# A hybrid retention and attention layer on one core: w_out's split pieces and the gate's vector-matrix product dealt out anew over the heads of the first sequence

## The chip, the core and the metric

One NeuronCore of a Trainium2 chip runs the whole program; the other cores are idle. The metric is the device time of one execution in microseconds (us), and the kernel before is given as the median of three runs. One further execution was profiled; all rows below are of that one. The engines are called as in the profile: PE is TensorE (matmuls; PEld is its weight load), DVE is VectorE, ACT is ScalarE, POOL is GpSimd, SP is SyncE, which here only issues transfers.

## What is computed

Two sequences, `x_prompt` (1024 tokens) and `x_sample` (512 tokens), pass through one layer with shared weights, in fp32. Cut to what matters here:

```python
mod = silu(c) @ w_ada + b_ada
shift, scale, gate = split(mod, 3)
h = rms_norm(x, norm_g) * (1 + scale) + shift
rq, rk, rv, rg, aq, ak, av, ag = split(h @ w_in)
ret_out = bidirectional_retention(rope(rq), rope(rk), rv, ...)
att_out = blocked_gqa(rope(norm(aq)), rope(norm(ak)), av)
mixed = concat([ret_out * silu(rg), att_out * silu(ag)]) @ w_out
y = x + gate * mixed
```

The two things that the change concerns are the last third of `mod`, the row `gate` (a vector of 1024 times a 1024 x 1024 part of `w_ada`, for both sequences at once), and the preparation of `w_out` (1024 x 1024).

## The kernel before

**Products in three parts.** A product in fp32 is made of three faster ones: each operand is split into a high part and a remainder (`hi`, `lo`), and `mm3` (lines 148 to 151) adds high x high, high x low and low x high in PSUM. A split of weights is a copy that rounds (line 139: ACT for `w_in`; line 143: POOL, through `pcopy`, for `w_out`) and a subtraction (line 140: POOL and DVE in turn for `w_in`, DVE for `w_out`).

**Order.** `sequence(1, 4, True)` runs the 512-token sequence first, then `sequence(0, 8, False)` the long one. In the first, the four retention heads 0 to 3 come one after another, and as a fifth turn (head 4) the key, value and first query projections of the attention. In turn `h` the projection of head `h` (`pqk`, `pvg`; 2 x 4 steps of 24 matmuls) is woven with the core of head `h - 1`, `ret_core`: state products `pst` from `vds`, transposes `pk` and `pq`, decayed queries `qd0s` and `qd1s` on DVE (line 716), scores `psc` and `sTs` (line 725), the output product `pos` (line 739), its norm (`sqs`, `sss`, then POOL's root `r_rets`, line 127), `mxs` (line 748) and the transposes of `mxs` (`pms`). Before a head's products can be used, its rotary products `rt1s` and `rt2s` on DVE are added by POOL (line 637).

**The gate's row.** `gate_mod` (lines 240 to 255) is a generator of 16 steps. Each loads a piece of `w_ada` of 256 KB, `gr`, through SP (line 247) into a ring of four raw buffers, and issues two matmuls (four as the profile counts them) into `pgm` (line 251). The weights of the next head, and of head 4, pass through the same ring. After eight steps half of the row is copied out by ACT (line 254). The table `GSTEPS` (line 314) says how many steps are taken in each turn; one extra step ends the generator. The row is first read by `load_gate`, at the end of head 4.

**w_out.** `split_wo` (lines 173 to 185) prepares one of eight pieces: SP loads 512 KB into `wor` (two buffers; line 178, or two halves by line 182), POOL copies it rounded into `woz` (line 143; two buffers `z`, WZ = 2), DVE subtracts (line 140), and POOL issues the write of 1 MB to `wod` in DRAM (line 185). The output stages read `wod` back much later. `WOH` (line 36) gives the number of pieces whose code stands at the end of each turn:

```python
    if first and h < RH:
        for j in range(sum(WOH[:h]), sum(WOH[: h + 1])):
            with tc.issue_after(acts["w"].ins):
                split_wo(wst, j)
```

**What sets the order.** The order in which instructions stand on an engine is settled when the program is built, by a scheduler that goes by its own estimate of when operands are ready; `issue_after` only keeps a piece's instructions behind the last weight load issued. So a piece written at the end of turn 0 or 1 can be placed anywhere after that load, among the instructions of the next turn. At run time each engine, and SP's queue of transfers, goes through its instructions strictly in that order.

Of the kernel before, what the change touches and what calls it, by code (L numbers as in the profile page):

```python
# [32 lines left out]
KO = 7  # L33
OUTLAG = 0
WZ = 2
WOH = (0,1,3,4)
LEAD = 5
PLEAD = 3
PTURN = -7
# [41 lines left out]
def hybrid_layer_kernel(ctx: ExitStack, tc: tile.TileContext, a: dict, y_prompt: bass.AP, y_sample: bass.AP):  # L81
# [175 lines left out]
    def merge(p, n, q, m):  # L257
        done = 0
        for i in range(n):
            if p is not None:  # L260
                next(p, None)
            while done * n < (i + 1) * m:
                next(q, None)
                done += 1
                yield
            yield
        for z in (p, q):
            if z is not None:
                yield from z
# [9 lines left out]
    def weave(units, n, steps, m, lead=0):  # L279
        done = 0  # L280
        for i, _ in enumerate(units):
            while steps is not None and done * (n - lead) < (i + 1 - lead) * m:
                if next(steps, steps) is steps:
                    steps = None
                done += 1
        if steps is not None:
            for _ in steps:
                pass
# [22 lines left out]
    def behind_ada():  # L311
        return tc.issue_after(adma[-1].ins)

    GSTEPS = {1: 7, 2: 7, 3: 3}

    def sequence(r, nt, first):
        tg = "ps"[r]
# [3 lines left out]
        with ExitStack() as sctx:  # L321
# [176 lines left out]
            with ExitStack() as rctx:  # L498
# [261 lines left out]
                def gates(pl, tag):  # L760
                    gs.extend(slot(f"g{tg}{i}") for i in range(2 * ng))
                    for jj in range(2):
                        segs = [(2816 + v * 256 + (2 * jj + i) * DH, DH) for i in range(2) for v in range(2)]
                        w = load_w(wring, f"wg{tg}{jj}", segs)
                        for g in range(ng):
                            for i in range(2):
                                pj = bank(f"pag{tg}{g}{jj}{i}")
                                wc = slice(i * P, (i + 1) * P)
                                c = slice(i * 512, (i + 1) * 512)
                                for k in range(KD):  # L770
                                    mm3(pj, w[:, k, 0, wc], w[:, k, 1, wc], hh[g][:, k, :], hl[g][:, k, :],
                                        k == 0, k == KD - 1)
                                    if k == 3:
                                        yield
                                silu_gate(pl, gs[g * 2 + jj][:, c], pj, [512], f"a{tg}{g}{jj}{i}", tag, 1)
                                yield
# [18 lines left out]
                for h in range(RH + 1):  # L795
# [3 lines left out]
                    else:  # L799
# [3 lines left out]
                        else:  # L803
                            units, n = gates(rp, "rt1"), 8 * ng
                    extra, m = itertools.islice(gsteps, GSTEPS.get(h, 0)) if first else iter(()), nsteps
                    if first:
                        m += GSTEPS.get(h, 0)
                    weave(units, n, merge(prev, nsteps, extra, m - nsteps), m + ((2, 3)[r] if h == RH else 0))
                    if h == 0:
                        decay_tables()  # L810
# [3 lines that stand above are left out]
# [320 lines left out]
```

## Time and profile before

| | |
|---|---|
| median of 3 runs | 959.81 us (958.32 to 961.81) |
| profiled execution, its own time | 958.77 us |
| its span, first to last instruction | 957.0 us |
| mean granted TensorE clock | 0.996 |
| busy: PE, DVE, POOL, ACT | 95%, 56%, 36%, 35% |

How to read it: busy time is a share of the whole span, while the stages differ. The cores of the first sequence's heads end with the `pms` rows at 97.64, 133.44 and 168.73 us (turns 1 to 3) and one more in turn 4; behind that lie the attention and output of the first sequence and the whole of the second. A row of the timeline shows start, duration, engine, line, operation, `out<-in`, the number of instructions merged, and in brackets the idle time of the engine just before, with what ended it. Matmul durations overlap one another, so stretches of PE are read from start to start.

### The profile page before, as it was taken

How to read it: one execution, taken by the hardware profiler on the slowest of the kernel's cores; microseconds unless marked ns; L12 is line 12 of the kernel's file. 1: busy time of each engine (PE TensorE's matmuls, PEld its weight loads, DVE VectorE, ACT ScalarE, POOL GpSimd, SP SyncE). 2: the span in 40 equal slices, each digit the busy share in tenths (PEclk: the TensorE clock that was granted, in tenths of full speed). 3: DMA queues.
4: the chain of work that ended last, by engine and by line, in shares of the span. 5: the costliest groups of instructions: out<-in, count | busy, mean ns of one | idle time of the engine just before them, and what ended most of it. 6: DMA issues, size and time to landing. Idle time of an engine off the chain costs nothing. (4 is left out here: it accounts for less than half of the span.)

```text
span 957.0 us, 15488 instructions
## 1 busy us (share of the span) xinstructions
PE 909.4 (95%) x6177; PEld 761.0 (80%) x6177; DVE 539.0 (56%) x1006; ACT 336.2 (35%) x582; POOL 344.7 (36%) x312
## 2 busy tenths in 40 slices
PE   4889998999999899999999999999998999999998
PEld 2778898997666799999999998899865666666666
DVE  2465555677764593543525344344997767666633
ACT  4353232343545452232122232232144433343331
POOL 4233454365326453232302211135563434242330
PEclk9999999999999999999999999999999999999999
DMA  9964778223732511111102111010027001101111
GB/s 272 278 184 144 253 212 295 77 46 133 308 153 89 185 47 45 46 46 45 29 17 46 45 45 44 26 51 7 12 80 293 24 22 44 45 23 45 45 45 44
DMA packets 95684, 92.99 MB, mean 97 GB/s; under 512 B 23502, under 2 KB 84858, under 8 KB 92540
## 3 DMA queue, kind: packets, MB, share of 16 engines
q1 hardware_dynamic: 92876, 77.85, 26.6%
q0 software_dynamic: 2736, 14.16, 3.7%
q8 instruction: 48, 0.79, 0.3%
q14 instruction: 24, 0.20, 0.1%
HBM read 77.30 MB, written 14.68 MB: 96 GB/s over the span
## 5 line engine op out<-in xcount | busy, mean ns | idle before, releaser
L925 ACT ACTIVATE pp<-pTp 128x1024 f32<-128x1024 f32 x64 | 65.6, 1026 | 122.8 <-PE pTp L922 113.6
L933 POOL TENSOR_TENSOR accp<-accp,pp 128x512 f32<-128x512 f32 x48 | 62.5, 1303 | 126.6 <-ACT pp L925 124.7
L870 DVE TENSOR_REDUCE nmhp<-pnp 128x2 f32<-128x1024 f32 x64 | 76.0, 1217 | 45.6 <-PE pnp L865 45.6
L149 PE MATMUL pvgp<-wvgp,hhp 128*128 128x256 f32 x224 | 65.0, 290 | 0.0
L149 PE MATMUL pqkp<-wqkp,hhp 128*128 128x256 f32 x224 | 64.6, 288 | 0.0
L150 PE MATMUL pvgp<-wvgp,hhp 128*128 128x256 f32 x224 | 64.3, 287 | 0.0
L151 PE MATMUL pvgp<-wvgp,hlp 128*128 128x256 f32 x224 | 63.9, 285 | 0.0
L151 PE MATMUL pqkp<-wqkp,hlp 128*128 128x256 f32 x224 | 63.7, 284 | 0.0
L150 PE MATMUL pqkp<-wqkp,hhp 128*128 128x256 f32 x224 | 63.4, 283 | 0.0
L149 PE MATMUL pyp<-wo,Mhp 128*128 128x512 f32 (+1 forms) x136 | 54.3, 399 | 7.6 <-DVE xrp L1019 7.6
L942 PE MATMUL pop<-pp,VVp 128*64 128x512 f32 x256 | 58.7, 599 | 0.0
L150 PE MATMUL pyp<-wo,Mhp 128*128 128x512 f32 (+1 forms) x136 | 51.6, 379 | 0.0
L151 PE MATMUL pyp<-wo,Mlp 128*128 128x512 f32 (+1 forms) x136 | 51.6, 379 | 0.0
L933 DVE TENSOR_TENSOR accp<-accp,pp 128x512 f32<-128x512 f32 x48 | 38.6, 804 | 15.8 <-ACT pp L925 15.1
L637 POOL TENSOR_TENSOR sp<-rt1p,rt2p 128x512 f32<-128x512 f32 x16 | 22.9, 1429 | 57.7 <-DVE rt2p L634 57.7
L149 PEld LDWEIGHTS pqkp<-wqkp,hhp 128*128 128x128 f32 x224 | 43.0, 192 | 0.0
L150 PEld LDWEIGHTS pqkp<-wqkp,hhp 128*128 128x128 f32 x224 | 42.9, 192 | 0.0
L151 PEld LDWEIGHTS pqkp<-wqkp,hlp 128*128 128x128 f32 x224 | 42.9, 191 | 0.0
L149 PEld LDWEIGHTS pvgp<-wvgp,hhp 128*128 128x128 f32 x224 | 42.8, 191 | 0.0
L150 PEld LDWEIGHTS pvgp<-wvgp,hhp 128*128 128x128 f32 x224 | 42.8, 191 | 0.0
L151 PEld LDWEIGHTS pvgp<-wvgp,hlp 128*128 128x128 f32 x224 | 42.8, 191 | 0.0
L942 PEld LDWEIGHTS pop<-pp,VVp 128*64 128x64 f32 x256 | 16.9, 136 | 32.4 <-issue 27.9
(458 smaller groups left out, 2799.3 us busy)
## 6 DMA issues: line engine op xcount, KB each, us to landing
wo<-wod SPq DMA_DIRECT2D x16, 1024.0 KB, 14.9
wa<-in_w_ada_dram SPq DMA_DIRECT2D x16, 512.0 KB, 5.9
wod<-woz POOLq DMA_DIRECT2D x8, 1024.0 KB, 6.6
gr<-in_w_ada_dram SPq DMA_DIRECT2D x16, 256.0 KB, 4.9
xn<-in_x_prompt_dram SPq DMA_DIRECT2D x8, 512.0 KB, 7.0
xrp<-in_x_prompt_dram SPq DMA_DIRECT2D x8, 512.0 KB, 3.6
out_dram<-xrp POOLq DMA_DIRECT2D x7, 512.0 KB, 2.9
xs<-in_x_sample_dram SPq DMA_DIRECT2D x4, 512.0 KB, 5.8
```

Source lines behind the costliest of these rows:

```text
L149: T.matmul(out, lh, rh, start=first, stop=False)
L150: T.matmul(out, lh, rl, start=False, stop=False)
L151: T.matmul(out, ll, rh, start=False, stop=last)
L637: G.tensor_tensor(qk, t1, t2, op=ALU.add)
L870: V.tensor_reduce(d["nmh"][:, n, 2 * pr : 2 * pr + 2], pn.rearrange("p (i k) -> p i k", i=2), AX.X, ALU.max, negate=True)
L925: d["exp", u] = S.activation(p, pT, AF.Exp)
L933: d["sum", v] = E.tensor_tensor(acc, acc, p[:, i * 512 : (i + 1) * 512], op=ALU.add)
L942: m = T.matmul(d["po"][v * DH : (v + 1) * DH, :], VV[:, 2 * kp + i, v, :], ps[v][:, i * 512 : (i + 1) * 512], start=(kp + i == 0), stop=(2 ...
```

## The change

Two tables get other numbers:

```diff
-WOH = (0,1,3,4)
+WOH = (2, 2, 2, 2)
...
-    GSTEPS = {1: 7, 2: 7, 3: 3}
+    GSTEPS = {1: 4, 2: 6, 3: 7}
```

No instruction is added or left out. The code of w_out's pieces stands two by two at the ends of turns 0 to 3, where it stood as none, one, three and four; the gate's sixteen products are done four, six and six in turns 1, 2 and 3, where it was seven, seven and two. What the scheduler makes of that is shown at three places.

POOL, from the end of turn 0 into turn 1. In the names, `ss0_1` is the rotated q and k of head 0, second pair of tiles, `woz2` and `wor2` are w_out's third piece, `wqks2r0` is the first raw piece of head 2's weights. Before:

```order
L637 TENSOR_TENSOR ss0_0_759<-rt1s0_0_761,rt2s0_0_762 128x512
L143 TENSOR_SCALAR woz0_1190<-wor0_1188 128x2x512
L637 TENSOR_TENSOR ss0_1_760<-rt1s0_1_770,rt2s0_1_771 128x512
L185 DMA wod0_60<-woz0_1190 128x2048
L637 TENSOR_TENSOR ss1_0_816<-rt1s1_0_919,rt2s1_0_920 128x512
L140 TENSOR_TENSOR wqks2_1196<-wqks2r0_1197,wqks2_1196 128x2x256
L637 TENSOR_TENSOR ss1_1_817<-rt1s1_1_1002,rt2s1_1_1003 128x512
L140 TENSOR_TENSOR wqks2_1196<-wqks2r2_1207,wqks2_1196 128x2x256
L125 TENSOR_SCALAR m_rets0_0_1112<-sss0_0_1110 128x4
L127 TENSOR_TENSOR r_rets0_0_1114<-m_rets0_0_1112,mhalf_71 128x4
```

Changed, from its third such row on:

```order
L143 TENSOR_SCALAR woz1_824<-wor1_822 128x2x512
L637 TENSOR_TENSOR ss0_1_760<-rt1s0_1_770,rt2s0_1_771 128x512
L185 DMA wod0_60<-woz0_818 128x2048
L185 DMA wod0_60<-woz1_824 128x2048
L637 TENSOR_TENSOR ss1_0_828<-rt1s1_0_931,rt2s1_0_932 128x512
L143 TENSOR_SCALAR woz2_1191<-wor2_1188 128x2x512
L140 TENSOR_TENSOR wqks2_1204<-wqks2r0_1205,wqks2_1204 128x2x256
L637 TENSOR_TENSOR ss1_1_829<-rt1s1_1_1010,rt2s1_1_1011 128x512
L140 TENSOR_TENSOR wqks2_1204<-wqks2r2_1215,wqks2_1204 128x2x256
L185 DMA wod0_60<-woz2_1191 128x2048
L143 TENSOR_SCALAR woz3_1198<-wor3_1195 128x2x512
L185 DMA wod0_60<-woz3_1198 128x2048
```

Where one piece stood between head 0's rotary sums, two stand now; the third and the fourth stand inside turn 1, the third ahead of head 1's second sum, and behind these rows the fifth comes ahead of the root `r_rets`.

DVE in turn 1, from head 1's second rotary product to the scores `sTs0_0` of head 0. Before:

```order
L634 TENSOR_TENSOR rt2s1_1_1003<-pqks1_1_942,rs_739 128x128 x4
L140 TENSOR_TENSOR wqks2_1196<-wqks2r1_1202,wqks2_1196 128x2x256
L716 TENSOR_TENSOR qd0s0_0_1025<-pqs0_0_1012,QD_752 128x512
L716 TENSOR_TENSOR qd1s0_0_1027<-pqs0_0_1012,QD_752 128x512
L140 TENSOR_TENSOR wqks2_1196<-wqks2r3_1212,wqks2_1196 128x2x256
L725 TENSOR_TENSOR sTs0_0_1063<-pscs0_0_1058,DT_751 128x512
```

Changed:

```order
L634 TENSOR_TENSOR rt2s1_1_1011<-pqks1_1_950,rs_739 128x128 x4
L140 TENSOR_TENSOR woz2_1191<-wor2_1188,woz2_1191 128x2x512
L140 TENSOR_TENSOR wqks2_1204<-wqks2r1_1210,wqks2_1204 128x2x256
L140 TENSOR_TENSOR wqks2_1204<-wqks2r3_1220,wqks2_1204 128x2x256
L716 TENSOR_TENSOR qd0s0_0_1033<-pqs0_0_1020,QD_752 128x512
L716 TENSOR_TENSOR qd1s0_0_1035<-pqs0_0_1020,QD_752 128x512
L725 TENSOR_TENSOR sTs0_0_1067<-pscs0_0_1062,DT_751 128x512
```

w_out's third piece and a second split of head 2's weights have moved ahead of `qd0s` and `qd1s`.

SP at the end of turn 2 and into turn 3; `wvgs3r3` is the last raw piece of head 3's weights, `gr1..` a piece of the gate's second half, `wkvs` the weights of head 4, and what a transfer waits for stands in brackets. Before:

```order
L164 DMA wvgs3r3_1627<-in_w_in_dram 128x2x128
L178 DMA wor4_1941<-in_w_out_dram 128x2x512 [waits DMAHW0_49]
L178 DMA wor5_1947<-in_w_out_dram 128x2x512 [waits DMAHW1_49]
L247 DMA gr112_1662<-in_w_ada_dram 128x2x256 [waits DMAHW3_49,DMAHW2_49,DVE_49]
L247 DMA gr113_1741<-in_w_ada_dram 128x2x256 [waits Pool_49]
L164 DMA wkvsr0_1974<-in_w_in_dram 128x2x256 [waits DMAHW5_49,DMAHW4_49,Pool_49]
```

Changed:

```order
L164 DMA wvgs3r3_1623<-in_w_in_dram 128x2x128 [waits PE_49]
L164 DMA wvgs3r3_1623<-in_w_in_dram 128x2x128
L182 DMA wor6_1953<-in_w_out_dram 64x2x512 [waits DMAHW6_49]
L182 DMA wor6_1953<-in_w_out_dram 64x2x512 [waits DMAHW7_49]
L182 DMA wor7_1960<-in_w_out_dram 64x2x512 [waits DMAHW0_49]
L182 DMA wor7_1960<-in_w_out_dram 64x2x512 [waits DMAHW1_49]
L247 DMA gr102_1658<-in_w_ada_dram 128x2x256 [waits DMAHW2_49,DVE_49]
L247 DMA gr103_1705<-in_w_ada_dram 128x2x256 [waits DMAHW3_49,Pool_49]
L247 DMA gr110_1741<-in_w_ada_dram 128x2x256 [waits DMAHW5_49,DMAHW4_49,DVE_49]
L247 DMA gr111_1796<-in_w_ada_dram 128x2x256 [waits Pool_49]
L247 DMA gr112_1832<-in_w_ada_dram 128x2x256 [waits DMAHW6_49,DMAHW2_49,PE_49]
L247 DMA gr113_1888<-in_w_ada_dram 128x2x256 [waits DMAHW7_49,DMAHW3_49,PE_49]
```

Six gate transfers, not two, now stand behind w_out's last two pieces (before, its fifth and sixth; the last two stood further on, among head 4's weights). On POOL the copy of `wor6` stands ahead of the split that frees the raw buffer of `gr103`.

## Rows read from the trace of the kernel before

**Rows 1.** The page, its span and its busiest engines.
```profile
span 957.0 us, 15488 instructions
PE 909.4 (95%) x6177; PEld 761.0 (80%) x6177; DVE 539.0 (56%) x1006; ACT 336.2 (35%) x582; POOL 344.7 (36%) x312
```

**Rows 2.** Waits of PE, 44 to 240 us: total, times, longest.
```profile
PE pgm L251 <- DMA gr<-in_w_ada_dram: 3.7, 4, 1.2
PE pos L739 <- DVE qd1s L716: 3.2, 1, 3.2
```

**Rows 3.** Timeline of PE, heads 1 to 3 (start, duration, what; idle before).
```profile
70.12 1.06 PE L251 MATMUL pgm<-gr,scT 128*32 128x256 f32 x12
72.08 0.63 PE L251 MATMUL pgm<-gr,scT 128*32 128x256 f32 x4 [0.90 <-DMA gr<-in_w_ada_dram]
73.64 0.63 PE L251 MATMUL pgm<-gr,scT 128*32 128x256 f32 x4 [0.94 <-DMA gr<-in_w_ada_dram]
74.20 0.71 PE L693 MATMUL psts<-vds,ss 128*128 128x128 f32 x4
...
88.91 0.38 PE L739 MATMUL pos<-R1s,qd1s 128*128 128x128 f32 x2
...
97.64 0.27 PE L501 MATMUL pms<-identr,mxs 128*128 128x128 f32 x1
...
133.44 0.27 PE L501 MATMUL pms<-identr,mxs 128*128 128x128 f32 x1
...
139.65 0.61 PE L693 MATMUL psts<-vds,ss 128*128 128x128 f32 x4
...
159.09 0.49 PE L739 MATMUL pos<-R1s,qd1s 128*128 128x128 f32 x2 [3.19 <-DVE qd1s L716]
...
168.73 0.27 PE L501 MATMUL pms<-identr,mxs 128*128 128x128 f32 x1
```

**Rows 4.** Busy time by stretch; PEclk is third from the right.
```profile
160.40:163.80 3.40, 3.40 (x19) 3.40 (x18) 1.30 (x2) 0.00 (x0) 0.59 (x1) 0.50 0.82 273
```

**Rows 5.** Timeline of POOL, heads 1 to 3.
```profile
71.53 1.05 POOL L143 TENSOR_SCALAR woz<-wor 128x1024 fp32r<-128x1024 f32 x1 [3.62 <-DMA wor<-in_w_out_dram]
72.54 1.26 POOL L637 TENSOR_TENSOR ss<-rt1s,rt2s 128x512 f32<-128x512 f32 x1
...
102.20 3.50 POOL L140 TENSOR_TENSOR wvgs<-wvgs2r,wvgs 128x512 fp32r<-128x512 f32 x2
...
149.44 1.05 POOL L143 TENSOR_SCALAR woz<-wor 128x1024 fp32r<-128x1024 f32 x1 [3.75 <-DMA wor<-in_w_out_dram]
```

**Rows 6.** Timeline of DVE, heads 1 to 3.
```profile
84.91 0.68 DVE L716 TENSOR_TENSOR qd1s<-pqs,QD 128x512 f32<-128x512 f32 x1
...
99.55 0.69 DVE L140 TENSOR_TENSOR wvgs<-wvgs2r,wvgs 128x512 fp32r<-128x512 f32 x1 [0.60 <-ACT wvgs L139]
...
102.27 2.30 DVE L140 TENSOR_TENSOR woz<-wor,woz 128x1024 fp32r<-128x1024 f32 x1 [2.03 <-POOL woz L143]
...
107.19 1.23 DVE L140 TENSOR_TENSOR woz<-wor,woz 128x1024 fp32r<-128x1024 f32 x1 [0.94 <-POOL woz L143]
...
154.23 3.61 DVE L140 TENSOR_TENSOR wkvs<-wkvsr,wkvs 128x512 fp32r<-128x512 f32 x1
```

**Rows 7.** Timeline of ACT, head 1.
```profile
71.53 0.51 ACT L677 ACTIVATE vds<-ss,kd 128x256 f32<-128x256 f32 x1
```

**Rows 8.** Line 182 (`wor`), loads of a piece's halves.
```profile
DMA to landing us min/median/max: 3.7/5.4/7.1
```

**Rows 9.** Line 185 (`wod<-woz`), writes of a piece of 1 MB.
```profile
DMA to landing us min/median/max: 4.5/6.6/9.2
```

**Rows 10.** Busy time by stretch, `pvgs` alone, head 3: PE, PEld, DVE, ACT, PEclk.
```profile
165.00:168.60 3.60, 3.60 (x31) 3.60 (x31) 0.00 (x0) 0.00 (x0) 1.00 0.30 109
```

**Rows 11.** Timeline of SP, weights of head 1.
```profile
54.30 5.72 SPq L164 DMA_DIRECT2D wvgs1r<-in_w_in_dram  x8
```

**Rows 12.** Line 247 (`gr`), loads of the gate's pieces.
```profile
DMA to landing us min/median/max: 2.7/4.9/6.7
```

## The prediction

> **What bounds it now.** The page first: TensorE (PE) is busy 95% of the span and no other engine above 56% [rows 1]. A PE that is nearly always busy runs through its instructions in their fixed order, so only what makes it wait, or slows it, can move the end. The view of who waited for whom, limited to PE and to 44 to 240 us, therefore comes second [rows 2]: two entries there concern the change, the gate's products (`pgm`) waiting for their transfers `gr`, 3.7 us in four waits, and one product of the retention core (`pos`) waiting 3.2 us for `qd1s` from VectorE (DVE). Third, PE's timeline shows where they stand [rows 3]: 0.90 and 0.94 in head 1, so the other two, 1.87, in head 2; and 3.19 at 159.09, in head 3. Fourth, the granted clock [rows 4]: for 3.40 us behind that last wait it is 0.50, the lower level (1.2 GHz of 2.4); half of 3.40 is 1.7 us lost. What the change can take away is thus 1.84 + 1.87 + 3.19 + 1.7 = **8.6 us**.
>
> The other engines matter through queues that are strictly in order. On GpSimd (POOL) a piece of w_out that has not landed holds up all behind it: idle 3.62 us before 71.53 and 3.75 before 149.44 [rows 5]. DVE's subtraction for a piece takes 1.23 us by itself and 2.30 beside a POOL instruction [rows 6].
>
> **The change, part by part.** No instruction is added or dropped; places change. Base: the profiled execution, 958.77 us (957.0 of span and 1.8 around it), 1.04 below the median 959.81.
>
> *Gate products.* Each is four matmuls, 0.56 us (73.64 to 74.20 [rows 3]). Head 1 does four instead of seven, head 2 six instead of seven, head 3 six instead of two: the sum stays. In head 1 the products that run behind one another are three: 70.12 + 1.06 [rows 3], so 71.2, where now it is 74.20. PE then wants `vds`, which ScalarE starts at 71.53 and has at 72.05 (0.51 [rows 7]): PE waits 0.9.
>
> *w_out in heads 0 and 1.* The order shows two pieces before the second half of head 0's rotary sum on POOL, three more inside head 1, the sixth as head 2 begins. The first lands as now (71.53); 1.05 each for two copies (L143 [rows 5]), some 0.4 for the second transfer, and 1.26 for the sum at 72.54 [rows 5] end at 75.3; PE wants it at 75.1. So 0.2 more, **1.1** in all (bounds 0 and 2.8: 1.7 more, if the second piece lands in 7.1 instead of the median 5.4 [rows 8]).
>
> Third piece: its buffer `z` (two exist) is free when the first has been written out: issued at 75.3, 6.6 to landing [rows 9], about 82.0. POOL copies it to 83.05 and goes on without a pause: a split, a sum, a split. DVE must take the piece, then two splits, then `qd0s` and `qd1s`. Two engines that both read SBUF alternate here, as at 102.20 (two POOL splits in 3.50) against 102.27 (2.30) [rows 5, 6]: 83.05 + 1.26 + 1.23 + 1.26 + 0.69 (the split at 99.55) + 1.26 + 0.69 + 2 x 0.68 (84.91) = 90.8, with 1.26 (72.54) for each of POOL's. PE is there at 88.91 - 2.15 + 0.2 = 87.0, since it left 72.05 instead of 74.20. Wait: **3.8**. From below: landing in 4.5 [rows 9], nothing alternating: 0. From above: landing in 9.2, 6.4. I take the median landing, as no row ties a quick or slow one to this place.
>
> The row gives 6.6 us for writing out a piece of 1 MB. The Trainium skill ("DMA: Bandwidth & Descriptors", Anatomy of one DMA) gives such a transfer of GpSimd's 2.0 us plus its bytes over 436 GB/s, an estimate of 4.4; by it this wait would be 1.6 and the sum -0.3. The trace's quickest, 4.5, is about that, its median is not, and the measured one stands in the sum.
>
> After it PE needs 97.64 - 88.91 - 0.56 = 8.2 to the transposes of `mxs` (one product less): 99.0. There the fifth piece stands before `r_rets` on POOL; its transfer is issued behind the next weights at about 91.2, lands 5.4 later, 1.05 and 1.3 for copy and root, then `mxs`: 99.4. If the clock falls behind the wait of 3.8, as it did behind that of 3.19, PE comes at 100.7 by itself. Between the two I take 100.0, against 97.64 now: **1.0** is added (bounds 0 and 1.7).
>
> *Head 2.* Its four gate transfers wait for splits that now come some 2 us later; the first lands about when wanted: **0.5** (0 to 1.9, as now). 133.44 - 97.64 = 35.80, less 1.87, less 0.56, plus 0.5: head 3's start falls at 133.9, now 133.44 [rows 3].
>
> *Head 3.* The piece in mid-head goes: the 3.19 and the 1.7 with it. But the gate's transfers stand on SP behind w_out's seventh and eighth piece, and the second waits for a raw buffer that POOL frees only after it has copied the seventh piece, which it waits for. The last weights are issued when head 2's sixth product is done, 24 matmuls (at 31 in 3.60 us [rows 10], 2.8) and a product before 133.9: 130.5. Two issues at 0.7 (eight in 5.72 [rows 11]), the piece's two halves at 0.6, landing 5.4 after the second is issued: 137.9. Copy 1.05, split 1.26, landing 4.9 [rows 12]: 145.2. PE wants it at 133.9 + 6.2 (133.44 to 139.65 [rows 3]), 0.6 for the state products there, 0.8 for seven matmuls and 0.56 for the product before: 142.1. Wait, with the smaller one of the product before it: **3.1** (quickest landings 3.7 and 2.7: 0; slowest 7.1 and 6.7: 6.6). Further on, scores (`sTs`) and squares (`sqs`) stand behind splits of `wkvs`, whose loads also moved: 0 to 3.2 (nearest row: 159.09), I take **1.0**, as those loads have two more projections as cover. Without the clock falling: 168.73 - 133.44 = 35.29, less 4.9, plus four products 2.2, plus 4.1: head 4's first transpose at 170.6, now 168.73.
>
> At nothing: the later end of the gate's row, covered by the k, v and q products that stand before its first use in load_gate; w_out's writes, read back in the output stage only. If those covers went, a product (0.56) or a landing (6.6) would show.
>
> **Sum:** -8.6 + 1.1 + 3.8 + 1.0 + 0.5 + 3.1 + 1.0 = **+1.9**. Own time 960.7; on the median's footing **961.7**.
>
> **Rivals.** *The transfers are quick.* With landings of 4.5 for writes, 3.7 and 2.7 for reads, the new waits shrink to 1.1, 1.7 (3.8 less 2.1), 0, 0.5, 0 and 0.5, together 3.8, and 8.6 - 3.8 = 4.8 come back: **955.0**. For it: no wait is then longer than the gate's 1.2 now, behind which no clock falls [rows 2], and the pieces are spread more evenly. Against: medians, not minima, fit the rows so far. By the rule on the Trainium skill's page "DMA: Bandwidth & Descriptors" named above, this rival would be the likelier one.
>
> *Slower: the gate's second transfer in head 3.* If the seventh piece lands in 7.1 and the gate's transfer in 6.7, the wait is 6.6 instead of 3.1 and the clock falls behind it (1.7 [rows 4]): +1.9 + 3.5 + 1.7 = +7.1, **966.9**. It decides where the two landings together pass 12 us, above their medians' 10.3. For it: POOL's own 3.75 of idle before 149.44. Against: no gate transfer waits that long now. The Trainium skill ("TensorE: Matmul & The Clock Gate", Part 1) says that idleness takes the clock to its lower level, by which a wait of this size costs its own length and that fall; the trace shows it once, at 160.40.
>
> *The waits only change places.* The new ones equal the old and the time stays within 1 us: **959.8**; the fixed order of PE favours it, nothing ties the sums together.
>
> **Numbers.** Forecast 0.5, quick 0.2, slower 0.2, same places 0.1. A change under 0.3% (2.9 us) can't be told from none. Quick gives faster, 0.20. The forecast's own range, 958.5 to 966, lies a little more below +2.9 than above: 0.28 of its 0.5 is same, 0.22 slower. Same 0.28 + 0.1 = 0.38; slower 0.22 + 0.2 = 0.42. The range 954.5 to 968 reaches just past the centres of both rivals, and so leaves out about half of each.
>
> **What would show it.** Right: no wait for `qd1s` in head 3 and none for `gr` in head 1; a wait of `pos` for `qd1s` of some 3 us near 87 to 91, POOL idle before the third and the fifth piece, a wait for `gr` near 142. Wrong: `qd1s` in head 1 in time, or gate transfers of head 3 landing before 142; then PE is ahead of its present place at 168.73. An end that moves with none of these waits would break the argument altogether.

## The result, and the profile after

The changed kernel takes 965.68 us (median of 8 runs, 962.1 to 969.5) against 960.28 for the kernel before (median of 8 runs, 958.32 to 961.81): a ratio of 1.0062, 95% interval 1.0037 to 1.0087. It is slower. The profiled execution took 965.12 us (before: 958.77). So 6.35 us have to be found between the two traces.

The page of the changed kernel shows the same work on every engine as [rows 1], in a longer span:

```profile
span 963.3 us, 15491 instructions
PE 914.3 (95%) x6177; PEld 763.4 (79%) x6177; DVE 539.1 (56%) x1006; ACT 335.8 (35%) x582; POOL 344.8 (36%) x312
```

Waits of PE from 44 to 240 us (total, times, longest), to be held against [rows 2]:

```profile
PE pms L501 <- DVE mxs L748: 6.1, 1, 6.1
PE pos L739 <- DVE qd1s L716: 3.2, 1, 3.2
PE p0s L149 <- ACT hhs L507: 2.0, 2, 1.4
PE psts L693 <- POOL woz L143: 1.0, 1, 1.0
```

No wait for `gr` is left, in any head. A wait for `mxs` of 6.1, which the kernel before does not have, is now the longest. PE's timeline, the rows that answer to [rows 3]:

```profile
69.88 1.06 PE L251 MATMUL pgm<-gr,scT 128*32 128x256 f32 x12
71.91 0.68 PE L693 MATMUL psts<-vds,ss 128*128 128x128 f32 x4 [0.97 <-POOL woz L143]
...
90.13 0.49 PE L739 MATMUL pos<-R1s,qd1s 128*128 128x128 f32 x2 [3.16 <-DVE qd1s L716]
...
104.47 0.47 PE L501 MATMUL pms<-identr,mxs 128*128 128x128 f32 x1 [6.10 <-DVE mxs L748]
...
140.45 0.38 PE L501 MATMUL pms<-identr,mxs 128*128 128x128 f32 x2
...
147.64 0.62 PE L251 MATMUL pgm<-gr,scT 128*32 128x256 f32 x4
148.99 0.62 PE L251 MATMUL pgm<-gr,scT 128*32 128x256 f32 x4
...
165.71 0.38 PE L739 MATMUL pos<-R1s,qd1s 128*128 128x128 f32 x2
...
174.78 0.27 PE L501 MATMUL pms<-identr,mxs 128*128 128x128 f32 x1
```

Against 97.64, 133.44 and 168.73 the first `pms` rows of the three cores stand 6.83, 7.01 and 6.05 later, and the span ends 6.3 later. Net, the whole loss stands at 104.47; behind it, heads 2 and 3 together win 0.8 back, though the clock costs some 2.2 there (below). What made `mxs` late is in POOL's timeline:

```profile
82.13 1.05 POOL L143 TENSOR_SCALAR woz<-wor 128x1024 fp32r<-128x1024 f32 x1 [2.94 <-DMA wod<-woz]
...
100.56 1.03 POOL L143 TENSOR_SCALAR woz<-wor 128x1024 fp32r<-128x1024 f32 x1 [7.89 <-DMA wor<-in_w_out_dram]
101.67 1.24 POOL L125 TENSOR_SCALAR m_rets<-sss 128x4 f32<-128x4 f32 x1
102.99 1.04 POOL L127 TENSOR_TENSOR r_rets<-m_rets,mhalf 128x4 f32<-128x4 f32 x1
```

and in DVE's:

```profile
95.44 0.69 DVE L743 TENSOR_REDUCE sss<-sqs 128x4 f32<-128x512 f32 x1 [3.31 <-ACT sqs L741]
101.62 1.22 DVE L140 TENSOR_TENSOR woz<-wor,woz 128x1024 fp32r<-128x1024 f32 x1 [5.49 <-POOL woz L143]
104.06 1.13 DVE L748 SCALAR_TENSOR_TENSOR mxs<-pos,r_rets,ss 128x128 f32<-128x128 f32 x4 [1.21 <-POOL r_rets L127]
```

The sum `sss` is there at 96.13. The root that needs it comes at 102.99, because POOL stands idle for 7.89 us before the fifth piece's copy, which is ahead of the root in its fixed order. PE could have gone on at 98.37 (104.47 - 6.10). The loads of the fifth and the sixth piece were issued by SP from 91.90 on, behind head 2's weights. The view of that line has one landing there, of the sixth piece, issued at 92.94 (microseconds to landing: least, median, most); the fifth's is not recorded, but POOL's copy of it starts 8.7 us after its issue at 91.90:

```profile
DMA to landing us min/median/max: 8.8/8.8/8.8
```

The view of the transfers from 88 to 101 us says what they shared the engines with, the writes of the third and fourth piece among it: 3.95 MB, where the kernel before moved 1.77 MB in the same 13 us. After and then before:

```profile
DMA packets 2462, 3.95 MB, mean 304 GB/s; under 512 B 159, under 2 KB 1695, under 8 KB 2204
```

```profile
DMA packets 2096, 1.77 MB, mean 136 GB/s; under 512 B 132, under 2 KB 1606, under 8 KB 2095
```

The clock falls within the wait and is at its lower level behind it (PEclk third from the right; [rows 4] are the same columns), some 2.2 us lost: half of 104.47 to 108, and 0.23 of the next two.

```profile
104.00:106.00 2.00, 1.53 (x7) 1.53 (x8) 1.94 (x6) 0.00 (x0) 1.97 (x4) 0.50 0.46 197
106.00:108.00 2.00, 2.00 (x12) 2.00 (x11) 2.00 (x1) 0.00 (x0) 2.00 (x2) 0.50 0.80 328
108.00:110.00 2.00, 2.00 (x15) 2.00 (x15) 2.00 (x3) 0.27 (x1) 0.15 (x1) 0.77 0.12 12
```

### The profile page after: what moved, and what is told of

The parts are those of the page before. It is cut to its first block, busy times and chain, and to the rows that moved or that the text cites. A ratio compares the mean times of both kernels' runs of the same rounds, so it can differ in the third digit from the quotient of the medians.

```text
span 963.3 us, 15491 instructions
## 1 busy us (share of the span) xinstructions
PE 914.3 (95%) x6177; PEld 763.4 (79%) x6177; DVE 539.1 (56%) x1006; ACT 335.8 (35%) x582; POOL 344.8 (36%) x312
```

## The experiments

**Theory A:** what costs the time is the place of pieces in the fixed orders of POOL and DVE, ahead of work that PE is about to need (head 0's root first of all). **Theory B:** it is the crowd of pieces and transfers in head 1, whatever the order. **Theory C:** it is the gate's products in head 3.

Single runs of one kernel lie up to 8 us from their median, so beside the time each trace gives a **stretch**: from the start of head 1's merged gate products (70.12 before) to head 4's first state product (172.05 before, row below). Before it is 101.93 us, in the changed kernel 178.10 - 69.88 = 108.22: 6.3 of the 6.35. The stretch is that of the profiled run. That run lies within 2 us of its kernel's median except in e2 (957.82, 3.1 below), e6 (961.07, 4.1 above and the slowest of its 12) and e10 (965.74, 3.2 below). The ratio is to the runs of the kernel before on the same chip.

```profile
172.05 0.61 PE L693 MATMUL psts<-vds,ss 128*128 128x128 f32 x4
```

| run | pieces, gate's steps | order of turn 2's pieces | stretch | us, median | ratio to before, 95% interval |
|---|---|---|---|---|---|
| before | 0,1,3,4; 7,7,3 | as scheduled | 101.93 | 959.8 to 961.2 | |
| change | 2,2,2,2; 4,6,7 | as scheduled | 108.22 | 965.68 | 1.0062 (1.0037 to 1.0087) |
| e1 | 2,2,2,2; 7,7,3 | as scheduled | 103.41 | 959.52 | 0.9988 (0.9962 to 1.0014) |
| e2 | 0,1,3,4; 4,6,7 | as scheduled | 102.31 | 960.95 | 1.0016 (0.9993 to 1.0038) |
| e3 | 2,2,2,2; 4,6,7 | behind the root | 105.75 | 963.13 | 1.0038 (1.0018 to 1.0059) |
| e4 | the same, three `z` | as scheduled | 105.53 | 964.53 | 1.0044 (1.0016 to 1.0072) |
| e5 | 2,2,2,2; 4,6,7 | behind root and splits | 102.75 | 958.37 | 0.9999 (0.9971 to 1.0026) |
| e6 | 0,1,3,4; 4,6,7 | behind the root | 103.09 | 956.97 | 0.9966 (0.9942 to 0.9991) |
| e7 | 0,1,3,4; 4,6,7 | behind root and splits | 97.50 | 955.29 | 0.9955 (0.9929 to 0.9982) |
| e8 | 2,2,2,2; 4,6,7, three `z` | behind root and splits | 96.97 | 955.10 | 0.9957 (0.9938 to 0.9976) |
| e9 | 0,1,3,4; 7,7,3 | behind root and splits | 101.37 | 960.06 | 0.9998 (0.9974 to 1.0022) |
| e10 | change, once more | as scheduled | 108.28 | 968.94 | 1.0081 (1.0056 to 1.0106) |

**e1, the pieces alone.** Of the change only the `WOH` line.

```diff
-WOH = (0,1,3,4)
+WOH = (2, 2, 2, 2)
```

> The pieces of w_out go two to each head as in the change, the gate keeps its seven, seven and two products of before in heads 1, 2 and 3. In this order head 0's root (r_rets) stands ahead of the fifth piece on POOL; in the changed kernel it stands behind it. Theory A (the loss is that place: the root waits for a piece that lands late, 6.1 us at 104.47, and the clock falls behind it for some 1.9): no wait of pms for mxs above 1.5, no fall of the clock at 100 to 110; the qd1s wait of head 1 shrinks from 3.2 to about 1.0, because the three products come back there (2.1 us); about 957 us, 8 below the change and 3 below before. Theory B (the crowd of pieces and transfers in head 1 costs the time in whatever order): the waits only move, 963 or more. Theory C (the gate's products in head 3 cost it): about 957 as well, but then the kernel with the gate's part alone is slower than before in head 3, not in head 1.

The time is that of before, neither A's 957 nor B's 963. In head 1 A's account of the root holds: no wait for `mxs`, no wait for `qd1s`, root at 96.46 and the fifth piece at 103.55, behind it. What A did not foresee stands in two places. Head 1 opens with a wait for `gr`, and the clock is at its lower level behind it (0.50 from 76 to 78 us), some 1.7 us lost:

```profile
73.58 0.63 PE L251 MATMUL pgm<-gr,scT 128*32 128x256 f32 x4 [1.71 <-DMA gr<-in_w_ada_dram]
```

And in head 3, with the piece in mid-head gone, but only two products there, PE waits 1.17 for `qd1s` and then

```profile
164.74 0.49 PE L739 MATMUL pos<-ss,sTs 128*128 128x128 f32 x2 [2.72 <-DVE sTs L725]
```

**e2, the gate's steps alone.** Of the change only the `GSTEPS` line.

```diff
-    GSTEPS = {1: 7, 2: 7, 3: 3}
+    GSTEPS = {1: 4, 2: 6, 3: 7}
```

> The pieces of w_out stay where they were before (none, one, three, four), only the gate's products move. In this order POOL has two pieces (the second and the third) ahead of head 0's root, which before stood ahead of both. Theory A: their loads are issued behind head 2's weights near 92 and land near 97 to 101, so the root comes near 101 to 103 and mxs near 104; PE wants it near 95 to 96, waits 6 us or more, and its clock falls: head 2 begins some 5 to 8 us later than before, end 963 to 968. Theory B (the crowd of pieces in head 1): only one piece is copied there before the root's place, so no such wait: 957 to 960. Theory C (the gate's products in head 3): head 1 gains up to 2, head 3 loses, its qd1s wait of 3.2 and a wait for gr: 960 to 964 with the loss behind 135 us.

POOL, the second and third piece ahead of the root:

```profile
92.39 1.04 POOL L143 TENSOR_SCALAR woz<-wor 128x1024 fp32r<-128x1024 f32 x1 [7.33 <-DMA wor<-in_w_out_dram]
93.69 1.90 POOL L143 TENSOR_SCALAR woz<-wor 128x1024 fp32r<-128x1024 f32 x1 [0.26 <-DMA wor<-in_w_out_dram]
...
98.03 1.04 POOL L127 TENSOR_TENSOR r_rets<-m_rets,mhalf 128x4 f32<-128x4 f32 x1
```

PE:

```profile
99.51 0.48 PE L501 MATMUL pms<-identr,mxs 128*128 128x128 f32 x1 [4.44 <-DVE mxs L748]
```

The wait for `mxs` is there, with the clock at its lower level behind it, though no piece is copied between 71.42 and 92.39, where the change copies three: B expected none. It is 4.4, not 6 or more (these transfers were issued at 86, not at 92), and 960.95 lies under the 963 of A and over the 960 of B. Head 2 begins 1.8 us later than before, counted from the stretch's start (29.30 against 27.52), and heads 2 and 3 win 1.4 of that back. C falls too: in head 3 there is no wait for `qd1s`, although a piece still stands in mid-head (copied at 152.69), and head 3 is 1.5 us shorter than before (135.41 to 172.52, against 133.44 to 172.05).

**e3, the root first.** The change, with the third turn's two pieces kept behind head 0's root.

```diff
-        G.tensor_tensor(r, m, mhalf[:, :n], op=ALU.pow)
+        acts["root", name] = G.tensor_tensor(r, m, mhalf[:, :n], op=ALU.pow)
...
-                            with tc.issue_after(acts["w"].ins):
+                            with tc.issue_after(acts["w"].ins), (tc.issue_after(acts["root", "rets0_0"].ins) if h == 2 else ExitStack()):
```

> The changed kernel, but the two pieces that the third turn issues stay behind head 0's root on POOL; on POOL and DVE the fifth piece changes places with the root's two steps and with mxs, the loads stay. Theory A: sss is there at 96.1, two steps of the root 2.3, a first mxs 1.1, so mxs is there near 99.5, PE comes at 98.4: a wait of about 1.2 instead of 6.1, without a fall of the clock. 4.9 and 1.9 come back: 958 to 959.5. Theory B: the load still lands near 100.6, and what stands behind it now, head 2's splits of wvgs, is late instead: a wait of 4 us or more near 108 to 112, end 963 or more.

Head 0's transposes come at 98.85 without a wait (A said 1.2), but the two pieces now hold the splits of head 2's weights. Those free the buffers for the gate's transfers, and a new wait stands in head 2, with the clock at its lower level behind it (0.53 from 110 to 112). PE:

```profile
98.85 0.27 PE L501 MATMUL pms<-identr,mxs 128*128 128x128 f32 x1
...
110.28 1.07 PE L251 MATMUL pgm<-gr,scT 128*32 128x256 f32 x4 [3.09 <-DMA gr<-in_w_ada_dram]
```

Counted from the stretch's start the transposes come 4.7 us earlier than in the change (29.88 against 34.59), of which 2.5 are left at its end. A named the cause of the wait; its sum was too good, for a new wait stands where B put one, and the median, 963.13, lies in B's range (963 or more) and not in A's (958 to 959.5). By time alone e3 can't be told from the change, as their intervals overlap; e5 below decides.

**e4, a third buffer.** `WZ = 3` in the changed kernel.

> The changed kernel with three buffers z instead of two, so the third piece need not wait for the first one to be written out. Theory A: the wait of pos for qd1s in head 1 (3.2 us) goes or falls under 1, but mxs still comes near 104, because the fifth piece's load is issued behind head 2's weights; the wait for mxs grows by what the other loses: 964.5 to 966, as the change. Rival (the copies waiting for z cost the time): 3 us or more are gained, 962 or less, and the fifth piece's load is issued earlier than 91.9 by about as much.

```profile
88.22 0.49 PE L739 MATMUL pos<-R1s,qd1s 128*128 128x128 f32 x2 [0.30 <-DVE qd1s L716]
...
102.86 0.47 PE L501 MATMUL pms<-identr,mxs 128*128 128x128 f32 x1 [6.38 <-DVE mxs L748]
```

The wait of 3.16 for `qd1s` is gone, so the buffer was its cause. The wait for `mxs` grew by 0.3 alone, not by all of it: the fifth piece's load is issued at 89.98, 2.5 earlier after the stretch's start than in the change, as the rival said, and the stretch is 2.7 shorter. The time does not confirm that: the median, 964.53, lies in A's range and not in the rival's (962 or less), and the intervals of e4 and of the change overlap.

**e5 to e8: behind the splits as well.** The pieces of the third turn stay behind the last splits of head 2's weights on POOL and DVE (`acts["lo", 0]` and `acts["lo", 1]` hold them); e3's hold on the root is not in this edit, as the root comes out ahead of those splits (at 99.43 against 102.58 in e5). In the kernels with 0,1,3,4 pieces the third turn has three, the second to the fourth, and all three are held. e5 is the change with it, e7 the gate's steps alone with it, e8 the change with three `z`; e6 is the gate's steps alone with e3's edit.

```diff
-        lo_eng.tensor_tensor(lo, src, hi.bitcast(F32), op=ALU.subtract)
+        return lo_eng.tensor_tensor(lo, src, hi.bitcast(F32), op=ALU.subtract)
...
-            split(S.copy, (G, V)[qt % 2], hi, lo, raw)
+            acts["lo", qt % 2] = split(S.copy, (G, V)[qt % 2], hi, lo, raw)
...
-                            with tc.issue_after(acts["w"].ins):
+                            with tc.issue_after(acts["w"].ins), ExitStack() as late:
+                                if h == 2:
+                                    late.enter_context(tc.issue_after(acts["lo", 0].ins))
+                                    late.enter_context(tc.issue_after(acts["lo", 1].ins))
```

> The changed kernel, but the two pieces that the third turn issues stay on POOL and DVE behind head 0's root and behind head 2's splits of wvgs as well. In the run with the root first the wait for mxs was gone, and a wait for gr of 3.1 with a fall of the clock stood in head 2 instead. Theory A (both waits have one cause: a piece in a fixed order ahead of work that PE is about to need, the second time ahead of the splits that free the buffers into which gr loads): neither wait, 4 to 5 us less than with the root first, 958 to 959, which is before's time. Theory B (head 1's transfers are too many for its time, in any order): gr or a later step waits 3 us or more all the same, 962 or more.

> The kernel with the gate's part alone, but the second and the third piece behind head 0's root, ahead of head 2's splits of wvgs. Theory A: the wait for mxs of 4.4 goes and its fall of the clock (some 2) too, and the pieces now hold the splits, so a wait for gr of 1 to 3 stands in head 2: 956 to 958.5. Theory B: as the gate's part alone, 960 to 962.

> The kernel with the gate's part alone, but the second and the third piece behind head 0's root and behind head 2's splits of wvgs. Theory A: the wait for mxs of 4.4 and its fall of the clock (some 2) go and nothing comes in their place before head 3: 954 to 955.5, faster than both kernels. Theory B: the loads are late whatever stands first, some other wait of 3 us or more appears in head 2: 958 or more.

> The changed kernel with three buffers z, and the two pieces of the third turn behind head 0's root and head 2's splits of wvgs. Theory A: no wait for mxs, none for gr, and none for qd1s in head 1 either (it was 0.3 with three buffers): some 3 us less than with two buffers and the same order, 955 to 956.5. Theory B (what the third buffer takes away comes back at the next step): as with two buffers, 958 or more.

All four medians lie in the range that A gave. e5 has neither the wait for `mxs` nor one for `gr` in head 2; e6 has the wait for `gr`, 1.96 in head 2, and one of 2.06 in head 3 that A did not name, each with the clock at its lower level behind it. In e8 the loads are as late as ever; the landing that is recorded is the sixth piece's, issued at 89.33:

```profile
DMA to landing us min/median/max: 8.9/8.9/8.9
```

It no longer matters, because POOL has passed root and splits before it needs the fifth piece's load (issued at 88.26):

```profile
92.88 1.04 POOL L127 TENSOR_TENSOR r_rets<-m_rets,mhalf 128x4 f32<-128x4 f32 x1
96.03 3.00 POOL L140 TENSOR_TENSOR wvgs<-wvgs2r,wvgs 128x512 fp32r<-128x512 f32 x2 [2.11 <-ACT wvgs L139]
99.00 2.50 POOL L143 TENSOR_SCALAR woz<-wor 128x1024 fp32r<-128x1024 f32 x2
```

This tells A from B. e5, too, has a landing of 8.9, with the pieces and buffers of the change, and its stretch is 5.5 shorter, its interval clear of the change's. With the same crowd and the same late load, the order decides whether PE waits. Both e7 and e8 are faster than both kernels.

**e9 and e10.** e9 is the kernel before with e7's order alone; e10 is the changed kernel again.

> The kernel before with only the order of its second and third piece changed: behind head 2's splits of wvgs (they were behind the root already, ahead of those splits). If the fixed place of the pieces is worth something without the gate's part, head 2's two waits for gr (1.87) go and it takes 957 to 958.5; the gate's part is then worth the other 2 to 3 us of the 955.3 that both together took. If it is only the gate's part that gains once the order is right: 959 to 960.5, as before.

> The changed kernel once more, for a profile and an interval beside the runs of this call: a wait for mxs of 4.5 to 6.5 and a fall of the clock behind it, 963 to 966.

e9 is at before's time: the two waits for `gr` in head 2 go, but one of 1.75 for `qd1s` comes there, with the clock at its lower level behind it (0.50 from 126 to 128), beside that of head 3. Waits of PE (total, times, longest):

```profile
PE pos L739 <- DVE qd1s L716: 4.1, 2, 2.3
```

So the order alone brings nothing that the time shows, and the gate's steps, once the order is right, bring 3.9 us of stretch (101.37 to 97.50). e10 repeats the loss: stretch 108.28, waits of 3.2 for `qd1s` and 4.7 for `mxs`. Its median is above the 966 expected.

## Why the prediction was right, and where its sum was not

The forecast was 961.7 in 954.5 to 968, with slower as the likeliest sign (0.42); the result is 965.68, slower. On the profiled execution it meant 960.7, and 965.12 came: 4.4 short. The sign was a close call (same had 0.38), and the range of 13.5 us held the result although two terms missed by more than 4 us, one up and one down. Of the signs that it named, the waits that were to go went, and the wait near 87 to 91 and POOL's idleness before the third and the fifth piece came; the wait for `gr` near 142 did not. By its steps, the terms of its sum in their order (the last one has two):

- **Removed, 8.6:** all of it went; of [rows 2] the waits for `gr` are gone, and that for `qd1s` is gone from head 3. For head 3 the reason given was wrong: "The piece in mid-head goes: the 3.19 and the 1.7 with it." e2 keeps that piece and has no such wait; e1 takes it away and has 1.17 and 2.72. Every run with the change's gate steps is without that wait and every run with the old ones has one (before, e1, e9): it is the four more gate products ahead of `pos` that gave DVE the time.
- **Step a, 1.1:** 0.97.
- **Step b, 3.8:** 3.16, with the third piece's copy at 82.13 (82.0 forecast) and `pos` at 90.13 (90.8). e4 shows the cause.
- **Step c, 1.0 with an upper bound of 1.7: the term that was mis-sized.** It named the mechanism, "the fifth piece stands before `r_rets` on POOL", and let it cost next to nothing. It measured a wait of 6.10. `mxs` was worked out for 99.4 and `pms` set at 100.0; it came at 104.47. Against 99.4: the issue 0.7 later (91.90), the landing 3.3 longer (8.7 to the copy's start, where the median 5.4 of [rows 8] was put in), the root's first step 1.1 longer (1.24; 0.19 in e8). The bound did not ask for a load beside two writes of 1 MB: even the slowest of [rows 8], 7.1, would have given 101.1. The trace of before held one, shown below this list: half a piece, issued beside two such writes, whose copy started 8.8 us after the issue. It is missing from [rows 8], as its landing is not recorded. A fall of the clock was weighed behind step b's wait; it came with this one and cost 2.2.
- **Step d, 0.5:** no wait. Head 2 took 35.98 (104.47 to 140.45); forecast 33.9, with the 0.5 in it. The clock's 2.2 covers the difference of 2.1; as the 0.5 did not come either, some 0.4 is lost elsewhere and stays unaccounted for.
- **Step e, 3.1 and 1.0:** neither came. The gate's second transfer in head 3 was issued at 146.09, 5.6 behind `pms` (6.4 in the forecast), and its product ran at 148.99 without waiting, so it landed in 2.9 at most, against 4.9; and no later step waited. This saved 4.1. Part went back: a product among projections cost 0.75 at the one place compared, not 0.56 (from the transposes `pqs` to the second `pvgs` matmul: 156.40 to 157.71 with a product between, 148.66 to 149.22 without one in the kernel before), which makes 0.8 for four. Head 3 took 34.33 where 36.7 was forecast, so some 1.0 more went back that stays unaccounted for.

The load of before that the bound missed, with the two writes ahead of it and beside it (SP's row first, then POOL's):

```profile
107.21 0.61 SPq L182 DMA_DIRECT2D wor<-in_w_out_dram  x1
107.11 0.62 POOL L185 DMA_DIRECT2D wod<-woz  x1
108.72 0.54 POOL L185 DMA_DIRECT2D wod<-woz  x1 [0.99 <-DVE woz L140]
115.98 1.05 POOL L143 TENSOR_SCALAR woz<-wor 128x1024 fp32r<-128x1024 f32 x1 [4.75 <-DMA wor<-in_w_out_dram]
```

Together: +4.5 (c) + 2.1 (head 2) - 2.4 (head 3) + 0.2 behind it is the 4.4. The rival for the slower side gave 966.9 for the gate's transfer in head 3; the time was near by luck, as no wait for `gr` came in head 3. What the prediction said for the quick rival, that no wait would then be longer than 1.2, does not fit its own list, which has one of 1.7; in e1 the clock fell behind one of 1.71.

On the rule weighed ahead of the sum: the Trainium skill ("DMA: Bandwidth & Descriptors", Anatomy of one DMA) gives GpSimd's transfer 2.0 us plus its bytes over 436 GB/s, an estimate of 4.4 us for a write of 1 MB. This trace does not agree: the write on which step b rests, issued at 75.22, landed in 6.8 us, and the two between 88 and 101 us in 6.4 at the median. So the measured value was the right one to put in.

## What to carry to other kernels

Ask of every background step what stands behind it on each in-order engine, and when that is wanted; then price the step by its slowest plausible transfer, with the traffic that the change itself puts beside it. A wait that is removed at one place can come back at the next thing held by the same step, as in e3 and e6, so move the step behind all of them: e7 and e8 gain 0.4% where the change as it was scheduled loses 0.6%. In a table like `GSTEPS`, read where the scheduler then puts the others: three gate steps fewer in head 1 put the pieces ahead of the root (e2; with the old steps, e1, the root stays ahead), and the wait for that root, 6.1, was the largest in the change.

## What the runs showed of the hardware that was not expected

A read of 512 KB took 8.8 to 9.0 us to land beside the two writes of 1 MB (the sixth piece in the change, e3, e4, e5, e8, e10), and 5.0 and 5.1 for the first and the fifth piece of the kernel before, issued at 66.36 and 132.61 beside no such write. Nearer to the change are e2, e6 and e7, where the same line's load is issued behind head 2's weights as well, but with no such write under way: 6.3 (issued at 86.01), 6.2 and 6.0. So the writes are the likely cause of the other 2.5 to 3 us; no run moved them alone.

The clock does not answer to the length of a wait alone. For the same `pos` behind the same wait for `qd1s`, 3.16 in the changed kernel left it at its upper level, 3.19 in e10 and 3.09 in e3 were followed by its lower one, and 2.59 in e5 by the longest fall of the four, from about 90 to 96.5 us. The changed kernel, then e5:

```profile
90.00:92.00 2.00, 1.87 (x15) 1.87 (x16) 2.00 (x4) 0.00 (x0) 0.00 (x0) 1.00 1.11 324
```

```profile
90.00:92.00 2.00, 1.75 (x8) 1.75 (x9) 2.00 (x4) 0.00 (x0) 0.08 (x1) 0.50 1.09 340
92.00:94.00 2.00, 2.00 (x11) 2.00 (x11) 0.26 (x1) 0.00 (x0) 0.56 (x1) 0.50 0.92 225
94.00:96.00 2.00, 2.00 (x12) 2.00 (x11) 0.00 (x0) 0.00 (x0) 0.00 (x0) 0.50 1.13 397
96.00:98.00 2.00, 2.00 (x17) 2.00 (x17) 0.00 (x0) 0.25 (x1) 0.00 (x0) 0.88 0.98 394
```

Shorter waits were followed by the lower level too, 1.71 in e1 and 1.75 in e9, while it did not come behind 2.72 in e1 or 2.33 in e9. So a wait of about 2 to 3 us costs its length and, at times, another 1.7 (e1, e3, e10) to 3.1 us (e5, from 90.25 on), summed from such stretches. In e5 wait and fall, less the 0.31 that e8 still waits there, are 5.4 of the 5.8 by which e8's stretch is shorter. What decides whether the clock falls stays open here.
